# Reworked norms between layers and a rebuilt side task in a one-core transformer kernel

## The chip, the cores and the metric

One NeuronCore of a Trainium2 chip runs the whole program in one launch. The metric is the device time of one execution in microseconds; the number to predict is the median over several executions. A profiled execution gives the trace, and a program reads views out of it: the page, groups of instructions, waits, the chain that ended last, timelines and windows.

## The reference

Sequence 512, width 1024, float32. Three layers follow one another, and each has a mixer and a feed-forward part. What matters here is the first layer's end, its feed-forward part, and the second layer's start:

```python
x = x + rms_norm(merged @ w_out, norm_mix_post)          # first mixer ends
h = rms_norm(x, norm_ffn_pre)
f = square(relu(h @ w_ff1)) @ w_ff2                      # 1024 -> 4096 -> 1024
x = x + rms_norm(f, norm_ffn_post)
h = rms_norm(x, mix_norm)                                # S5 mixer begins
u = h @ ssm_w_in
# per group: x_l = a*x_{l-1} + B u_l (complex), y = Re(C x), then gelu and a gated product
```

`rms_norm` divides by the root of the mean square over the 1024 features of a token. In the kernel tokens lie along the free axis and features on the partitions, so a mean over features is a sum over partitions and over eight tiles.

## The kernel before

Activations are eight tiles of 128 features by 512 tokens. Each float32 product runs as three passes of split operands (high by high, low by high, high by low): `passes` (L226). Weights come as a stream (class `Stream`, L78): SyncE's queue loads 512 KB at a time (`wraw`, three buffers, L107), ScalarE rounds 512 columns to the high half (`whi`), and VectorE subtracts to get the low half (`wlo`), each with four buffers. For the streams named in `POOL_SPLITS` (L55: `w_s5in`, `w_gdn`) GpSimd does the subtraction. One product of a 1024-long contraction (`dense`) is 24 matmuls of 512 columns.

Tile, the framework, orders each engine's instructions at compile time by program order and its own estimate of when operands are ready, and sets the semaphores. Two engines are kept from one PSUM bank at the same time.

**Norms.** `token_sums` (L332) multiplies the tile of summed squares with a column of ones, four token blocks, and for two accumulators it interleaves them block by block; `rms_cols` (L342) turns the sums into reciprocal roots with tiny VectorE operations (`rsqrt`, L295, two steps of third order); `spread_ps` (L359) brings them back to every partition by four matmuls with the identity. A float32 matmul is two records in the trace, a transpose one.

**Norms between layers.** `post_norm` (L909) runs twice, after the first mixer and after the first feed-forward part. For each of eight blocks VectorE multiplies by the spread root and adds the old x (`x`), ScalarE makes the high half of the next input and VectorE its low half (`h`), ScalarE squares x and GpSimd adds the squares up (`pre_block`, L927). Then comes the next layer's first group of four outputs, block by block (`dense_group`, L276): 96 matmuls.

**Feed-forward part with a side task.** `ffn_relu2` (L949) does four quarters of eight 24-matmul outputs of `w_ff1` and eight of `w_ff2`. After most outputs `pump` (L191) takes one piece of `s5_prepare` (L1066), a generator that makes the S5 matrices: exact exponentials and sines, then in two halves (`s5_half`, L1120) the powers B a^n on VectorE and C a^n on GpSimd with `cmul` (L1019), six operations each on real and imaginary tiles, and for each of eight blocks (`s5_block`, L1160) expansions on ScalarE, transposes and products on TensorE, and seven doublings of a table of rotations `s5e`, six operations each. Results go to DRAM by SyncE's queue (`s5m`). The generator has 63 pieces; 61 pumps take place, and the rest is run out after the last output, before `post_norm`.

**S5 mixer.** `s5_layer` (L1235): first group, `pre_scale` (L936), then a pipeline of `s5_in`, `s5_scan`, `s5_states`, `s5_out` over eight blocks with round trips through DRAM.

Of the kernel before, what the change touches and what calls it, by code (L numbers as in the profile page):

```python
# [9 lines left out]
F32 = mybir.dt.float32  # L10
# [6 lines left out]
P = 128  # L17
# [37 lines left out]
POOL_SPLITS = ("w_s5in", "w_gdn")  # L55
# [74 lines left out]
class Kern:  # L130
# [164 lines left out]
    def rsqrt(self, m, shape, tag="", out=None):  # L295
# [6 lines left out]
        self.ts(yi, yi, 0x5DCB8400, ALU.add)  # L302
        for step in range(2):
            self.stt(a, y, (64.0 / 9.0) ** (2 - step), y, ALU.mult, ALU.mult)
            self.tt(a, a, m, ALU.mult)
            self.stt(a, a, -10.0 / 3.0, a, ALU.add, ALU.mult)
            if step == 1 and out is not None:
                self.stt(out, a, 5.0, y, ALU.add, ALU.mult)
            else:
                self.stt(y, a, 5.0, y, ALU.add, ALU.mult)  # L310
        return y if out is None else out
# [20 lines left out]
    def token_sums(self, accs, ps=None):  # L332

        if ps is None:
            ps = self.ps("s")
        for c in range(4):
            for i, acc in enumerate(accs):
                self.mm(ps[:, c:c + 1], acc[:, c * P:(c + 1) * P], self.ones[:acc.shape[0], 0:1],
                        start=(i == 0), stop=(i == len(accs) - 1))
        return ps  # L340

    def rms_cols(self, accs, n, scale=None):  # L342
# [4 lines left out]
        if scale is None:  # L347
            self.ts(m, ps[:, 0:4], 1.0 / n, ALU.mult, EPS, ALU.add)
        else:
            self.stt(m, ps[:, 0:4], 1.0 / n, scale, ALU.mult, ALU.mult)  # L350
            self.tt(m, m, scale, ALU.mult)
            self.ts(m, m, EPS, ALU.add)
        rs = self.cp.tile([P, 4], F32, name="rs_cols", tag="rs_cols", bufs=2)
        self.rsqrt(m, (P, 4), out=rs)
        if scale is not None:
            self.tt(rs, rs, scale, ALU.mult)
        return rs
# [44 lines left out]
    def first_norm(self):  # L402
# [19 lines left out]
        self.rs = self.rms_cols([acc], D)  # L422
# [486 lines left out]
    def post_norm(self, wo, accs, gain, old, gain_next, keep=True, scale=None):  # L909


        ps = self.spread_ps(self.rms_cols(accs, D, scale))
        rsb = self.cp.tile([P, T], F32, name="rsb", tag="rsb", bufs=1)
        self.act(rsb, ps)
        acc = self.tmp("acc")
# [8 lines left out]
        self.pre_acc = acc  # L924
        return xs, hs

    def pre_block(self, x, gain, acc, first, eng=None):  # L927
# [5 lines left out]
        self.sq_acc(acc, x, first, eng)  # L933
        return hi, lo

    def pre_scale(self):  # L936
        self.rs = self.rms_cols([self.pre_acc], D)
        self.rsb = self.spread(self.rs)

    def pre_norm(self, x, gain=None):  # L940
        acc = self.tmp("acc")
        hs = [self.pre_block(x[k], gain and self.col(gain, k), acc, k == 0) for k in range(KB)]
        self.pre_acc = acc
# [5 lines left out]
    def ffn_relu2(self, x, hs, gain_post, gain_next, side):  # L949
# [3 lines left out]
        rs = self.rms_cols([self.pre_acc], D)  # L953
        rs2 = self.cp.tile([P, 4], F32, name="rs2", tag="rs2", bufs=1)
        self.tt(rs2, rs, rs, ALU.mult)
# [24 lines left out]
        return self.post_norm(part, accs, gain_post, x, gain_next, scale=rs2)  # L980
# [38 lines left out]
    def cmul(self, out_r, out_i, ar, ai, br, bi, t1, t2, eng=None, conj=False):  # L1019

        eng = eng or self.nc.vector
        self.tt(out_r, ar, br, ALU.mult, eng)
        self.tt(t1, ai, bi, ALU.mult, eng)
        self.tt(out_r, out_r, t1, ALU.add if conj else ALU.subtract, eng)
        self.tt(out_i, ar, bi, ALU.mult, eng)
        self.tt(t2, ai, br, ALU.mult, eng)
        self.tt(out_i, out_i, t2, ALU.subtract if conj else ALU.add, eng)

    def exp_exact(self, out, x):

        n, r, q, e = (self.small() for _ in range(4))
        M = 12582912.0
        xc = self.small()
# [13 lines left out]
        for h in (e, n):  # L1047
            i = self.small().bitcast(I32)
# [17 lines left out]
    def s5_prepare(self):  # L1066
# [12 lines left out]
        self.exp_exact(step, ls)  # L1079
        yield  # L1080
        self.tt(t1, lr, step, ALU.mult)
        self.exp_exact(dec, t1)
# [33 lines left out]
        yield  # L1116
        for hf in range(2):
            yield from self.s5_half(hf, fr, fi, ar, ai, sn, cs)

    def s5_half(self, hf, fr, fi, ar, ai, sn, cs):  # L1120
# [5 lines left out]
        sh = [P, NP, K]  # L1126
        v = lambda t: t.rearrange("p (a k) -> p a k", k=K)
        b3 = lambda t: t[:, ps_].unsqueeze(2).to_broadcast(sh)
        tb, tc_ = ([v(t[:, 0:W]), v(t[:, W:2 * W])] for t in (self.slot("sy", name="s5t") for _ in range(2)))
# [5 lines left out]
        br, bi = v(raw[0][:, 0:W]), v(raw[0][:, W:])  # L1135
        cr, ci = v(raw[1][:, 0:W]), v(raw[1][:, W:])

        big = lambda: self.pool.tile([P, 4 * W], F32, name="s5pw", tag="s5pw", bufs=4)
# [689 lines left out]
```

## Time and profile before

| | us |
|---|---|
| median of 3 runs | 2289.0 |
| lowest, highest run | 2287.34, 2297.26 |
| the profiled execution | 2291.0 |
| its span, first to last instruction | 2289.1 |

In the profiled execution TensorE's mean granted clock is 0.977 of full speed. Start times in the rows count from the span's start. In a timeline, a line's time covers the first start to the last end of the instructions merged in it, and matmuls overlap their neighbours; the chain's times don't overlap.

### The profile page before, as it was taken

Reading aid. Unit: us, or ns where it says so; the run is one execution under the profiler, and the core shown is the slowest. Engines: PE = TensorE matmul, PEld = TensorE weight load, DVE = VectorE, ACT = ScalarE, POOL = GpSimd, SP = SyncE. Lnnn points to the kernel's source line nnn. Section 1 sums busy time; section 2 is a strip of 40 time slices with the busy share of each in tenths; the row PEclk is TensorE's granted clock in tenths of the full one; section 3 lists DMA queues with packets and bytes.
Section 4 is the critical chain, followed back from the end, with each engine's and each line's share of the span. In section 5 each row is a group of like instructions: output and inputs, shape, how many; then the busy total and the mean of one; then the engine's idle time right before and its main releaser. Section 6 shows DMA issues by size and latency. Waiting matters only on the chain.

```text
span 2289.1 us, 29097 instructions
## 1 busy us (share of the span) xinstructions
PE 2163.4 (95%) x10538; PEld 1806.3 (79%) x10538; DVE 1439.0 (63%) x2977; ACT 998.8 (44%) x1902; POOL 366.4 (16%) x400
## 2 busy tenths in 40 slices
PE   8999999999979999997789999999998899999999
PEld 6778878888867888886577788888878777888887
DVE  6678746677559557667584554355479897543542
ACT  4443336666434544463222433233357665332331
POOL 4123201111023002103451000000025541000000
PEclk9999999999989999998889999999999999999999
DMA  4211133335423444442674333333321112333332
GB/s 150 89 45 38 42 97 102 107 114 186 132 65 89 138 138 125 139 143 88 196 224 123 89 95 92 102 92 102 90 63 35 35 46 65 93 94 100 96 98 92
DMA packets 87985, 231.62 MB, mean 101 GB/s; under 512 B 10145, under 2 KB 19873, under 8 KB 87841
## 3 DMA queue, kind: packets, MB, share of 16 engines
q1 hardware_dynamic: 75168, 208.60, 30.1%
q10 hardware_dynamic: 12672, 21.16, 3.0%
q8 instruction: 83, 1.36, 0.2%
q14 instruction: 62, 0.50, 0.1%
HBM read 202.46 MB, written 27.26 MB: 100 GB/s over the span
## 4 chain that ended last, share of the span: by engine, by line
PE 76%; DVE 16%; ACT 3%; issue 2%; POOL 2%; DMA 1%; ACTq 0%; SPq 0%; DVEq 0%; POOLq 0%
PE ps_d L231 64%; PE ps_p L263 3%; PE ps_p L231 3%; PE ps_s L263 2%; PE ps_z L231 2%; DVE t L205 1%; DVE wlo L205 1%; PE ps_s L243 1%; DVE s5t L205 1%; DVE s5pw L205 1%; DVE x L212 1%; DVE h L212 1%; PE ps_p L839 1%; DVE mp L1619 1%; ACT sb_e L215 0%
## 5 line engine op out<-in xcount | busy, mean ns | idle before, releaser
L231 PE MATMUL ps_d<-h,whi 128*128 128x512 f32 (+1 forms) x3152 | 1003.8, 395 | 22.9 <-ACT h L215 10.6
L215 ACT ACTIVATE whi<-wraw 128x512 fp32r<-128x512 f32 (+1 forms) x648 | 402.4, 625 | 740.0 <-PE ps_d L231 634.9
L231 PEld LDWEIGHTS ps_d<-h,whi 128*128 128x128 f32 (+1 forms) x3152 | 595.5, 189 | 149.8 <-ACT h L215 11.6
L205 DVE TENSOR_TENSOR wlo<-wraw,whi 128x512 fp32r<-128x512 f32 x569 | 399.4, 705 | 388.4 <-ACT whi L215 383.9
L231 PE MATMUL ps_d<-h,wlo 128*128 128x512 f32 (+1 forms) x1576 | 621.6, 394 | 6.0 <-DVE wlo L205 5.1
L231 PEld LDWEIGHTS ps_d<-h,wlo 128*128 128x128 f32 (+1 forms) x1576 | 299.1, 190 | 67.9 <-DVE wlo L205 6.0
L231 PE MATMUL ps_d<-fh,wlo 128*128 128x512 f32 x608 | 237.2, 390 | 4.9 <-DVE wlo L205 4.9
L231 PE MATMUL ps_d<-fh,whi 128*128 128x512 f32 x608 | 237.6, 391 | 0.0
L231 PE MATMUL ps_d<-fl,whi 128*128 128x512 f32 x608 | 236.7, 389 | 0.0
L205 DVE TENSOR_TENSOR t<-ps_d,rsb 128x512 f32<-128x512 f32 x136 | 92.9, 688 | 127.4 <-PE ps_d L231 123.5
L231 PEld LDWEIGHTS ps_d<-fh,wlo 128*128 128x128 f32 x608 | 114.2, 188 | 30.3 <-DVE wlo L205 7.0
L231 PEld LDWEIGHTS ps_d<-fl,whi 128*128 128x128 f32 x608 | 114.1, 188 | 23.7
L231 PEld LDWEIGHTS ps_d<-fh,whi 128*128 128x128 f32 x608 | 114.2, 188 | 23.4
L205 POOL TENSOR_TENSOR wlo<-wraw,whi 128x512 fp32r<-128x512 f32 (+3 forms) x79 | 100.6, 1279 | 159.8 <-ACT whi L215 158.3
L1618 POOL MEMSET mp<- 128x128 f32 x32 | 6.6, 211 | 465.2 <-PE ps_d L231 444.3
L215 ACT ACTIVATE fh<-t 128x512 fp32r<-128x512 f32 x76 | 48.0, 631 | 66.0 <-DVE t L205 54.4
L205 DVE TENSOR_TENSOR fl<-t,fh 128x512 fp32r<-128x512 f32 x76 | 53.0, 697 | 31.9 <-ACT fh L215 30.2
L231 PE MATMUL ps_d<-whi,c 128*128 128x256 f32 (+1 forms) x224 | 53.3, 321 | 4.6 <-DVE v L212 3.6
L231 PE MATMUL ps_d<-os,whi 128*128 128x512 f32 x128 | 46.7, 420 | 8.6 <-DVE v L212 6.3
L215 ACT ACTIVATE t<-ps_d 128x512 f32<-128x512 f32 (+1 forms) x42 | 25.0, 596 | 59.0 <-PE ps_d L231 57.6
L205 POOL TENSOR_TENSOR acc<-acc,t 128x512 f32<-128x512 f32 x14 | 23.0, 1644 | 153.6 <-ACT t L215 153.5
L205 DVE TENSOR_TENSOR x<-ps_d,x 128x512 f32<-128x512 f32 x56 | 38.3, 687 | 14.4 <-PE ps_d L231 14.1
(411 smaller groups left out, 3373.1 us busy)
## 6 DMA issues: line engine op xcount, KB each, us to landing
wraw<-in_w_gu SPq DMA_DIRECT2D x88, 512.0 KB, 3.5
wraw<-in_w_ff SPq DMA_DIRECT2D x64, 512.0 KB, 3.6
wraw<-in_w_dn SPq DMA_DIRECT2D x44, 512.0 KB, 3.6
wraw<-in_w_gates SPq DMA_DIRECT2D x24, 512.0 KB, 3.6
wraw<-in_w_glu SPq DMA_DIRECT2D x16, 512.0 KB, 3.5
wraw<-in_w_sc SPq DMA_DIRECT2D x12, 512.0 KB, 3.4
gsc<-t SPq DMA_DIRECT2D x24, 256.0 KB, 2.0
sg<-gsc SPq DMA_DIRECT2D x24, 256.0 KB, 3.6
```

What stands on the lines that cost most here:

```text
L205: self.note((eng or self.nc.vector).tensor_tensor(out=out, in0=a, in1=b, op=op))
L212: (eng or self.nc.vector).scalar_tensor_tensor(out=out, in0=a, scalar=s, in1=b, op0=op0, op1=op1)
L215: self.note(self.nc.scalar.activation(out, a, fn, **kw))
L231: self.note(self.nc.tensor.matmul(ps, lhsT=a, rhs=b, start=(start and n == 0), stop=(stop and n == 3 * len(ops) - 1), skip_group_check=loose))
L243: self.note(self.nc.tensor.matmul(o, lhsT=v(h, j), rhs=x, start=(j == 0 and i == 0), stop=(j == n - 1 and i == 1)))
L263: self.nc.tensor.matmul(ps, lhsT=lhsT, rhs=rhs, start=start, stop=stop)
L839: self.nc.tensor.matmul(self.sb_at(z, i), lhsT=self.tri if j == i else self.neg, rhs=self.sb_at(s, j), start=False, stop=(j == i and n == ...
L1618: nc.gpsimd.memset(p[b][:, c0 + n:c0 + n + P], 0.0)
L1619: nc.vector.tensor_tensor_reduce(out=p[b][:, cs], in0=z[b][:, cs], in1=wide[:, 4 * P - n:], scale=1.0, scalar=-3e38, op0=ALU.add, op1=ALU. ...
```

## The change

- **Reciprocal roots.** `rms_cols` works on the plain sum (the factor 1024 goes into the constants), and `rsqrt` takes one step of third and one of second order: nine operations where there were ten. In the norm after the feed-forward part three operations on the mean and a last multiplication become one addition of a column `offset`, made early.
- **Sums and spread.** `token_sums` goes accumulator by accumulator, so the four products of the first don't stand behind the second; `spread_ps` uses transposes.
- **`post_norm`.** `keep_warm` issues ten 128-column float32 matmuls on constants after the sums and eight after the spread, in both uses. The first block's multiplication stands before ScalarE's copy of the spread. The squares and their sum leave the loop: `pre_sums` does them after the next layer's first group, on ScalarE and VectorE.
- **`w_s5in`** is split on VectorE.
- **Side task.** `cmul2` keeps real and imaginary part side by side in a tile: two multiplications over both, one subtraction, one addition, all on VectorE; GpSimd has no part in powers. Doublings 0 to 3 are made once for all 32 pairs in a new table `s5eb`; each block copies its part into `s5e` (one buffer of 128 x 1024) and does doublings 4 to 6. The pieces are cut anew: 58 pieces for 61 pumps. In a block, both transposes and the products now stand in one piece, and so do the diagonal term and the second expansions.

```diff
-POOL_SPLITS = ("w_s5in", "w_gdn")
+POOL_SPLITS = ("w_gdn",)
...
+        self.stt(a, y, 64.0 / 9.0 / (k * k), y, ALU.mult, ALU.mult)
+        self.tt(a, a, m, ALU.mult)
+        self.stt(a, a, -10.0 / 3.0, a, ALU.add, ALU.mult)
+        self.stt(y, a, 5.0, y, ALU.add, ALU.mult)
+        self.stt(a, y, -0.5 / (k * k), y, ALU.mult, ALU.mult)
+        self.tt(a, a, m, ALU.mult)
+        out = y if out is None else out
+        self.stt(out, a, 1.5, y, ALU.add, ALU.mult)
...
-        for c in range(4):
-            for i, acc in enumerate(accs):
-                self.mm(ps[:, c:c + 1], ...
+        for i, acc in enumerate(accs):
+            for c in range(4):
+                self.note(self.nc.tensor.matmul(ps[:, c:c + 1], ...
...
+    def keep_warm(self, n):
+        if n:
+            ps = self.ps("d")
+            with self.tc.issue_after(self.last_on(self.nc.tensor)):
+                for _ in range(n):
+                    self.note(self.nc.tensor.matmul(ps[:, 0:P], lhsT=self.ones, rhs=self.ident, start=True, stop=True))
...
-            self.mm(ps[:, c * P:(c + 1) * P], cols[:, c:c + 1].to_broadcast([P, P]), self.ident)
+            self.note(self.nc.tensor.transpose(ps[:, c * P:(c + 1) * P], cols[:, c:c + 1].to_broadcast([P, P]),
+                                               self.ident))
...
+        cols = self.rms_cols(accs, offset)
+        self.keep_warm(warm[0])
+        ps = self.spread_ps(cols)
+        self.keep_warm(warm[1])
         rsb = self.cp.tile([P, T], F32, name="rsb", tag="rsb", bufs=1)
-        self.act(rsb, ps)
...
             self.tt(o, o, rsb if m else ps, ALU.mult)
+            if m == 0:
+                self.act(rsb, ps)
...
-            hs.append(self.pre_block(new, self.col(gain_next, m), acc, m == 0, self.nc.gpsimd))
+            hs.append(self.pre_block(new, self.col(gain_next, m)))
...
+    def pre_sums(self, x):
+        self.pre_acc = self.tmp("acc")
+        for k in range(KB):
+            self.sq_acc(self.pre_acc, x[k], k == 0)
...
+    def cmul2(self, out, a, fr, fi, t1, t2):
+        self.tt(t1, a, fr, ALU.mult)
+        self.tt(t2, a, fi, ALU.mult)
+        self.tt(out[:, 0], t1[:, 0], t2[:, 1], ALU.subtract)
+        self.tt(out[:, 1], t1[:, 1], t2[:, 0], ALU.add)
...
+    def s5_double(self, e, k, pairs, sn, cs):
+        n, w = 1 << k, pairs.stop - pairs.start
+        o = (k + 1) * 32 + pairs.start
+        fac = [q[:, o:o + w].unsqueeze(1).unsqueeze(3).to_broadcast([P, 2, w, n]) for q in (cs, sn)]
+        self.cmul2(e[:, :, :, n:2 * n], e[:, :, :, 0:n], *fac, *self.s5_scratch(w, n))
...
-                self.cmul(pw(Cr, n), pw(Ci, n), b3(ar), b3(ai), prev[0], prev[1], *tc_, nc.gpsimd)
+                self.cmul2(pw(C, n), prev, b3(ar), b3(ai), *self.s5_scratch(NP, K))
...
+        et = self.pool.tile([P, 2 * T], F32, name="s5e", tag="s5e", bufs=1)
+        e = et.rearrange("p (x a c) -> p x a c", x=2, a=4)
+        nc.vector.tensor_copy(out=e[:, :, :, 0:16], in_=self.s5eb[:, :, m * 4:m * 4 + 4])
+        self.s5_double(e, 4, slice(m * 4, m * 4 + 4), sn, cs)
...
+        self.s5_double(e, 6, slice(m * 4, m * 4 + 4), sn, cs)
+        nc.sync.dma_start(out=dst[:, 5 * T:7 * T], in_=et)
...
         first = self.dense_group(st, hs, "ddpp")
+        self.pre_sums(x)
         self.pre_scale()
```

## Rows read from the trace of the kernel before

**Rows 1.** the page, part 1: busy us of each engine (share), instructions
```profile
PE 2163.4 (95%) x10538; PEld 1806.3 (79%) x10538; DVE 1439.0 (63%) x2977; ACT 998.8 (44%) x1902; POOL 366.4 (16%) x400
```

**Rows 2.** windows by stage; columns in the first line
```profile
core 0: us, PE busy (x) PEld busy (x) DVE busy (x) ACT busy (x) POOL busy (x), PEclk, DMA share, GB/s
...
645.00:675.00 30.00, 18.69 (x75) 15.45 (x75) 24.29 (x37) 12.41 (x22) 9.49 (x6) 0.74 0.06 18
...
675.00:1046.00 371.00, 366.08 (x1710) 304.19 (x1711) 241.70 (x678) 181.33 (x348) 52.64 (x74) 0.99 0.42 130
...
1046.00:1094.00 48.00, 34.34 (x133) 27.34 (x131) 35.55 (x84) 17.93 (x35) 19.40 (x19) 0.79 0.25 75
...
1094.00:1230.00 136.00, 103.91 (x541) 87.89 (x541) 96.73 (x119) 31.12 (x62) 58.90 (x53) 0.87 0.65 197
```

**Rows 3.** chain that ended last, first feed-forward part: start, us, what
```profile
757.23 0.87 PE ps_p L1187 x8
...
771.24 21.81 PE ps_d L231 x96
```

**Rows 4.** timeline, TensorE, first norm between layers: start, us, what, [idle <- releaser]
```profile
645.43 2.62 PE L263 MATMUL ps_s<-ones,acc 128*128 128x1 f32 x14 [1.61 <-ACT acc L215]
...
655.86 0.79 PE L231 MATMUL ps_d<-h,whi 128*128 128x512 f32 x1 [3.43 <-ACT h L215]
...
674.87 0.80 PE L231 MATMUL ps_d<-h,wlo 128*128 128x512 f32 x1 [5.12 <-DVE wlo L205]
...
687.45 0.95 PE L263 MATMUL ps_s<-ones,acc 128*128 128x1 f32 x8
```

**Rows 5.** timeline, VectorE, the same stretch
```profile
648.09 0.16 DVE L209 TENSOR_SCALAR rms_m<-ps_s 128x4 f32<-128x4 f32 x1 [2.51 <-PE ps_s L263]
...
650.08 0.16 DVE L212 SCALAR_TENSOR_TENSOR rs_cols<-rq_a,rq_y 128x4 f32<-128x4 f32 x1
...
654.30 1.41 DVE L212 SCALAR_TENSOR_TENSOR x<-wo,cols,xin 128x512 f32<-128x512 f32 x2
...
674.13 1.28 DVE L205 TENSOR_TENSOR wlo<-wraw,whi 128x512 fp32r<-128x512 f32 x2
```

**Rows 6.** windows of 1 us; columns as before, PEclk third from the end
```profile
646.00:647.00 1.00, 1.00 (x7) 1.00 (x7) 0.00 (x0) 0.00 (x0) 0.00 (x0) 0.52 0.65 74
...
659.00:660.00 1.00, 1.00 (x4) 0.83 (x3) 1.00 (x2) 0.00 (x0) 0.94 (x1) 0.65 0.00 0
...
1052.00:1053.00 1.00, 0.96 (x5) 0.96 (x6) 0.00 (x0) 0.00 (x0) 0.00 (x0) 0.61 0.68 262
```

**Rows 7.** timeline, TensorE, second norm between layers
```profile
1044.52 1.95 PE L263 MATMUL ps_p<-sz 128*128 128x128 f32 x16
...
1046.30 1.84 PE L263 MATMUL ps_s<-ones,acc 128*128 128x1 f32 x16
...
1093.68 0.95 PE L263 MATMUL ps_s<-ones,acc 128*128 128x1 f32 x8
```

**Rows 8.** timeline, VectorE, the same stretch
```profile
1066.22 1.48 DVE L205 TENSOR_TENSOR s5e<-s5e,s5et 128x256 f32<-128x256 f32 x1
...
1078.87 1.75 DVE L212 SCALAR_TENSOR_TENSOR h<-x,cols,h 128x512 fp32r<-128x512 f32 x1
```

**Rows 9.** waits of TensorE, 688 to 1044 us: total us, times, longest
```profile
PE ps_d L231 <- DVE wlo L205: 4.9, 4, 1.4
```

**Rows 10.** windows, first feed-forward part: coefficient powers, then what follows
```profile
719.00:742.00 23.00, 20.59 (x88) 16.06 (x87) 23.00 (x30) 6.57 (x12) 20.42 (x24) 1.00 0.24 70
...
742.00:902.00 160.00, 160.00 (x764) 133.95 (x763) 92.05 (x284) 81.72 (x160) 1.64 (x9) 1.00 0.45 142
```

**Rows 11.** DMA issues, 690 to 1070 us: count, KB each, us to landing
```profile
s5m<-s5e SPq DMA_DIRECT2D x16, 256.0 KB, 2.0
```

**Rows 12.** waits of SyncE's DMA queue, 690 to 1044 us
```profile
SPq L107 <- DVE wlo L205: 169.6, 46, 11.8
```

**Rows 13.** timeline, TensorE, the kernel's start
```profile
1.10 4.47 PE L263 MATMUL ps_s<-ones 128*128 128x128 f32 x24 [1.10 <-DVE ones L384]
```

More of the change, by code (lines that the diff above doesn't have):

```diff
@@ L301, in rsqrt @@
         self.ts(yi, m.bitcast(I32), 1, ALU.logical_shift_right, -1, ALU.bitwise_xor)
[L302 to L311, printed above, removed]
+        self.ts(yi, yi, self.GUESS[k], ALU.add)
+        self.stt(a, y, 64.0 / 9.0 / (k * k), y, ALU.mult, ALU.mult)
[6 more added lines that the diff above has]
+        self.stt(out, a, 1.5, y, ALU.add, ALU.mult)
+        return out
     def sq_acc(self, acc, src, first, eng=None):
@@ L922, in post_norm, with pre_block @@
             xs.append(new)
-            hs.append(self.pre_block(new, self.col(gain_next, m), acc, m == 0, self.nc.gpsimd))
-        self.pre_acc = acc
+            hs.append(self.pre_block(new, self.col(gain_next, m)))
         return xs, hs
-    def pre_block(self, x, gain, acc, first, eng=None):
+    def pre_block(self, x, gain):
         hi, lo = self.slot("h", F32R), self.slot("h", F32R)
@@ L932, in pre_block @@
             self.split_scaled(hi, lo, x, gain)
-        self.sq_acc(acc, x, first, eng)
         return hi, lo
+    def pre_sums(self, x):
+        self.pre_acc = self.tmp("acc")
+        for k in range(KB):
+            self.sq_acc(self.pre_acc, x[k], k == 0)
     def pre_scale(self):
-        self.rs = self.rms_cols([self.pre_acc], D)
+        self.rs = self.rms_cols([self.pre_acc])
         self.rsb = self.spread(self.rs)
     def pre_norm(self, x, gain=None):
-        acc = self.tmp("acc")
-        hs = [self.pre_block(x[k], gain and self.col(gain, k), acc, k == 0) for k in range(KB)]
-        self.pre_acc = acc
+        self.pre_acc = self.tmp("acc")
+        hs = []
+        for k in range(KB):
+            hs.append(self.pre_block(x[k], gain and self.col(gain, k)))
+            self.sq_acc(self.pre_acc, x[k], k == 0)
         return hs
@@ L1017, in small, with exp_exact @@
         return self.sm_tile[:, o:o + 32 * n]
[L1019 to L1031, printed above, removed]
+    def cmul2(self, out, a, fr, fi, t1, t2):
[3 more added lines that the diff above has]
+        self.tt(out[:, 1], t1[:, 1], t2[:, 0], ALU.add)
+    def exp_exact(self, out, x, scratch):
+        n, r, q, e, xc, *two = scratch
         M = 12582912.0
-        xc = self.small()
         self.ts(xc, x, 100.0, ALU.min, -115.0, ALU.max)
@@ L1046, in exp_exact @@
         self.tt(n, n, e, ALU.subtract)
-        for h in (e, n):
-            i = self.small().bitcast(I32)
+        for h, t in zip((e, n), two):
+            i = t.bitcast(I32)
             self.ts(i, h, 127.0, ALU.add, 8388608.0, ALU.mult)
@@ L1078, in s5_prepare @@
         step, dec, t1, t2 = (self.small() for _ in range(4))
-        self.exp_exact(step, ls)
+        scratch = [self.small() for _ in range(7)]
+        self.exp_exact(step, ls, scratch)
         yield
         self.tt(t1, lr, step, ALU.mult)
-        self.exp_exact(dec, t1)
+        self.exp_exact(dec, t1, scratch)
         self.tt(t1, dec, dec, ALU.mult)
@@ L1125, in s5_half @@
         W = NP * K
[L1126 to L1129, printed above, removed]
+        v = lambda t: t.rearrange("p (x a k) -> p x a k", x=2, k=K)
+        b3 = lambda t: t[:, ps_].unsqueeze(1).unsqueeze(3).to_broadcast([P, 2, NP, K])
         raw = [self.slot("sy", name="s5raw") for _ in range(2)]
@@ L1154, in s5_half @@
         for b in range(4):
-            for _ in self.s5_block(hf * 4 + b, b, Br, Bi, Cr, Ci, cr, ci, sn, cs):
+            if b == 0:
+                next(c_pw)
+            for _ in self.s5_block(hf * 4 + b, b, B, C, v(raw[1]), sn, cs):
                 if b == 0:
```

105 lines of the change are left out of this document (48 added, 57 removed).

## The prediction

> **What bounds the kernel now.** I read the page's busy shares first, then windows by stage, then the chain, and last the timelines of two engines around the two norms between layers. TensorE is busy 95% of the span [rows 1], so a gain has to come from the few places where it stands or runs slowly. The stages show where [rows 2]: around the first norm it is busy 18.7 of 30 us at a mean granted clock of 0.74, around the second 34.3 of 48 at 0.79, in the S5 pipeline 103.9 of 136 at 0.87. In the feed-forward part between them it is busy 366.1 of 371 us: little is to be had there, whatever the side task costs the others.
>
> A first group of a layer is 96 matmuls, which take 21.8 us at full clock [rows 3]. From the first norm's waiting sums to the end of that group 42.0 us go by (645.43 to 687.45) [rows 4]; from the last output's end in the feed-forward part to the end of the S5 group it is 49.2 (1044.52 to 1093.68) [rows 7]. So some 20 and 25 us stand around the matmuls. Three things fill them. Small VectorE operations run one by one, 0.2 us each: eleven from 648.09 to 650.25 [rows 5]. The loop on VectorE is slowed where GpSimd works beside it: a half that takes 0.67 takes 1.75, a 256-wide doubling 1.48 [rows 5, 8]. And the clock is at its lower level (1.2 GHz) part of the time: at 646 us it falls after TensorE had stood for 1.6 us, and rises at 659.6, 3.8 us after the group began [rows 4, 6].
>
> **First norm.** Unchanged: the second accumulator is ready at 645.43 [rows 4]. The four products of the first one now stand before that, so eight records are left behind it: 0.9 us at full clock (16 in 1.84 [rows 7]), 1.5 at the lower one (14 in 2.62 [rows 4]). Then ten small operations instead of eleven, 2.0 us. Beside them run the ten fillers: the start of the kernel has twelve of their size in 4.47 us at the lower clock [rows 13], so ten take 3.7; at full clock a record costs 0.115, so 2.3. The spread is four transposes, 0.44 (eight in 0.87 [rows 3]), with 0.15 of hand-over. If the clock holds, VectorE starts at 645.43 + 0.9 + 2.0 + 0.6 = 648.9. If it falls at 646.0 as before and rises 3.8 us later, the fillers end at about 650.3 and the loop starts at 650.9; if it doesn't rise in time, at 651.8.
>
> The loop is eight blocks of one multiplication (0.60, as the paired subtractions at 674.13) and two three-operand operations (0.67, [rows 5]), without GpSimd beside it: 15.5 us. TensorE, fed every 1.9 us, needs 2.73 for a block, so it would be the bound. But VectorE also makes `wlo`, and the order shown by the trace puts the fifth block's `wlo` behind nearly the whole loop: 674.13, after the last x, with TensorE standing 5.12 us for it [rows 4, 5]. I take that order as kept. It is ready 14.7 us after the loop starts; TensorE has done its four prepared blocks about 13 us after, stands 1.7, and needs 10.9 for the other four. The group ends 25.6 us after the loop's start: 674.5 with the clock held, 676.5 with the fall, 677.4 at the worst. The gain is 13.0, 11.0 or 10.0. I take **11.0**, since in the nearest row the clock is down before the first filler could begin.
>
> The fillers take `d` banks whose readers are done, and what is queued behind them on TensorE is the spread, then the group; the price of that is in the three cases. ScalarE's copy of the spread now waits for the first multiplication, which only the second block needs: nothing, as VectorE has the first block's addition meanwhile.
>
> The Trainium skill, TensorE: Matmul & The Clock Gate, section "What's actually happening", has the activity monitor's window run free of the kernel, so that a fall can come at another moment in another run. By that 674.5 and 676.5 are both open, 2 us apart; no run here tells which.
>
> **Second norm.** The last output ends at 1044.52, and the side task's tail follows on TensorE [rows 7]. That tail (16 records and four transposes, 2.2 us) moves ahead of the last outputs, where TensorE is full: the end comes at 1046.7. As before the first norm 1.6 us pass until the second accumulator is there; then 0.9, ten operations at 0.2 (fourteen before), 0.6: the loop starts at 1051.8. Gone from this stretch is what ran between: the doublings of the last block, one of them 1.48 us long [rows 8], and GpSimd's sums and splits. GpSimd's `wlo` of this stream becomes VectorE's, and with the order above the same wait of 1.7 us appears here, new. The group ends 25.6 us after: 1077.4, against 1093.68: **16.3**. Here I take the clock as held: before, it stayed full from 1044.5 to 1052 [rows 6], though with the tail as work. If it falls, 2 to 3 us less.
>
> Behind both groups stand the squares and sums: eight on ScalarE, seven additions of 0.60 on VectorE, 4.2 us. VectorE has the time while TensorE does the last four blocks, so they cost nothing as long as the loop holds its 15.5 us; if not, the sums wait, TensorE's queue with them, and in the S5 part the spread root that every `s5_in` needs: up to 4 us at each place. There the way from group to spread root itself gets an operation and four records shorter: **0.6**.
>
> **Side task.** TensorE waits for VectorE 4.9 us in four waits [rows 9], all where powers run on both engines: VectorE is full 23.0 of 23 us, GpSimd 20.4 [rows 10]. With four operations in place of six, a product is about 1.9 us uncontended (two of 512 columns at 0.60 [rows 5], two of half that, which I estimate at 0.35), and sixteen are 30 us spread over 61 pumps; the largest piece (two products, a copy and a doubling) is 4.7 us of an interval of 5.5, a quarter of the 96 matmuls. Outside the powers VectorE was busy 92 of 160 us, doublings included [rows 10], 3.1 in an interval; so this piece overshoots by some 2, under the cover of four prepared `wlo`, 10.9 us of TensorE. So the 4.9 come back. Against it: three PSUM tiles in one piece on two `p` banks, so the products wait for ScalarE's copy of the first transposes. No row shows that wait; where these pieces stood apart, TensorE was busy 160.0 of 160 us [rows 10], which is the lower end, 0; the upper is a copy of 512 columns and its hand-over, 1 us as ScalarE's part of the 1.6 before the sums [rows 4]. As other matmuls can be ordered between, I take 0.2 for each of eight blocks: 1.5. Net **3.4**, ends 4.9 and -3.1.
>
> **The rest.** 16 other reciprocal roots, 0.2 us each, a third of them where someone waits: **1.2** (0 to 3.2). Spreads at three other norms, four records less each: **1.3** (0 to 1.5). `w_s5in` on VectorE in the pipeline, eight splits: 4.8 us on an engine busy 96.7 of 136 [rows 2], against eight fewer on GpSimd, each of which could slow a VectorE operation by 1 us. Between -4.8 and +8 I take 0, as chain and relief share the same stretch.
>
> The Trainium skill, TensorE: Matmul & The Clock Gate, section "Terms", gives the transpose mode as four times faster for float32. The row has it at twice (0.87 for eight against 1.84 for sixteen). By the page a spread would be 0.2 us shorter, six times, and the sum 1.3 lower.
>
> **Sum.** 11.0 + 16.3 + 0.6 + 3.4 + 1.2 + 1.3 = 33.8. The profiled execution took 2291.0, so 2257.2; it lies 2.0 above the median of the runs, which leaves **2255**.
>
> **Rivals.**
> *Fillers that don't hold the clock.* It falls in both norms, the fillers run at the lower level and the spread stands behind them. For it: the fall at 646.0 precedes them, and twelve such records at the start ran at the lower clock [rows 13]. Against: rises within 3.8 us of work. Price: 1 and 3 us: 2259.
> *The gain given back in S5.* The sums come late or the additional splits sit on the chain of scans: 4 + 4.8 us, and 4 more at the first norm: 2268. For it: VectorE is on that chain, and the sums now depend on it. Against: the additions fit beside TensorE's last four blocks.
> *The loop meets its splits.* The framework's order changes and `wlo` comes in time at both norms (3.4), GpSimd's absence quickens S5 (up to 8): 2246.
> *Slower.* The single `s5e` buffer: the copy for block m+1 waits until block m's 512 KB are in DRAM, and VectorE's queue, `wlo` first, stands behind it. The stores land in 2.0 us [rows 11], but on SyncE's queue a weight load can wait up to 11.8 us [rows 12] and hold a store behind it. The cover is 10.9. If each of seven copies lost 7 us, the 3.4 would not come and 49 would be lost: 2255 + 3 + 49 = 2307. It begins to cost at a landing 16.4 us after the doubling (an interval and the cover) and turns the sign at about 22; the rows speak for 2 to 14.
> *It doesn't do what it says*, a piece of the side task still standing in the second norm: 5 us, 2260.
>
> **Chances.** Forecast and tail piece (2250 to 2262) 0.52, clock 0.13, given back 0.18, better 0.12, slower 0.05 (with others of its sign). The ends of the unknown costs reach 2240 and 2272, and this range leaves less than 2 in 10 out. A measurement of this kernel can tell about 0.5%, 11 us. Faster by more (under 2277.6): 0.91; within: 0.06; slower: 0.03.
>
> **What would show it.** In the profile after: a first group ending about 25 us after the loop's start; no GpSimd beside the loops; the window clock at 1.0 through the second norm; no side-task operation behind the last output; TensorE full from 688 on; a wait on `wlo` in the middle of both groups. Wrong it would be if halves still took 1.7 us without GpSimd, if TensorE stood for the sums behind a group, if pieces with three PSUM tiles showed waits on ScalarE, or if the S5 part grew by what the norms gave.

## The result, and the profile after

The changed kernel takes 2261.92 us (median; 2261.87 to 2263.37), the kernel before 2288.55 in the runs beside it: the ratio is 0.9877, with an interval of 0.9852 to 0.9902. So it is faster by 1.2%, clear of the runs' spread, 7 us behind the forecast of 2255 and inside the range. The profiled execution of after took 2261.87 us (span 2260.0, mean granted clock 0.981), that of before 2291.0: 29.1 between the two traces. In two later sets of runs the changed kernel took 2260.7 and 2258.95, beside 2289.1 and 2288.29 of before.

Stages are cut here where TensorE starts the products of a norm's sums (the second accumulator's at the first norm; at the second norm the first accumulator's, which before the change stand together with the second's and now 1.6 us ahead of them). The page's first part and windows at these cuts, of the kernel after; the columns are us, busy us (instructions) of TensorE, its weight load, VectorE, ScalarE, GpSimd, then the granted clock and DMA. The order is mixer, first norm to the end of its group, feed-forward part, second norm to the end of its group, S5 part, second feed-forward part, MLA, third:

```profile
PE 2161.9 (96%) x10586; PEld 1808.0 (80%) x10586; DVE 1416.0 (63%) x2778; ACT 1001.7 (44%) x1902; POOL 278.1 (12%) x308
```

```profile
33.66:647.77 614.11, 588.35 (x3083) 494.05 (x3081) 417.27 (x750) 302.82 (x553) 101.06 (x119) 0.99 0.29 95
647.77:679.15 31.38, 29.47 (x144) 25.11 (x145) 27.27 (x51) 16.69 (x27) 3.50 (x9) 0.95 0.21 68
679.15:1033.70 354.55, 354.45 (x1673) 294.61 (x1672) 224.67 (x517) 178.59 (x344) 0.00 (x0) 1.00 0.40 134
1033.70:1066.34 32.64, 30.41 (x154) 25.97 (x153) 25.87 (x47) 16.96 (x31) 0.36 (x4) 0.95 0.32 107
1066.34:1285.56 219.22, 186.70 (x910) 155.60 (x909) 146.77 (x188) 64.18 (x118) 48.47 (x46) 0.92 0.50 157
1285.56:1642.10 356.54, 355.66 (x1573) 292.00 (x1572) 174.22 (x300) 125.90 (x221) 1.78 (x4) 1.00 0.29 93
1642.10:1917.34 275.24, 248.83 (x1437) 215.96 (x1436) 227.39 (x675) 173.75 (x412) 107.21 (x111) 0.94 0.15 48
1917.34:2260.00 342.66, 338.93 (x1501) 280.30 (x1499) 154.15 (x235) 105.55 (x167) 0.00 (x0) 1.00 0.30 96
```

Against before, by the same cuts (the third to the fifth are differences of starts in [rows 4] and [rows 7], the others are read from the same timeline of before):

| stage | before | after | difference | predicted |
|---|---|---|---|---|
| start | 34.02 | 33.66 | -0.4 | in "the rest" |
| mixer | 611.41 | 614.11 | **+2.7** | in "the rest" |
| first norm and group | 42.02 | 31.38 | -10.6 | -11.0 |
| feed-forward part | 358.85 | 354.55 | -4.3 | |
| second norm and group | 47.38 | 32.64 | -14.7 | with the line above -19.7 |
| S5 part | 223.93 | 219.22 | **-4.7** | -0.6 |
| second feed-forward part | 357.21 | 356.54 | -0.7 | in "the rest" |
| MLA | 270.93 | 275.24 | **+4.3** | in "the rest" |
| third feed-forward part | 343.35 | 342.66 | -0.7 | in "the rest" |

"The rest" was put at -2.5 and came to +5.2. The first norm came out as worked out, the second together with the feed-forward part. First TensorE's timeline around the first norm (start, us, what, idle before and its releaser), which answers [rows 4]:

```profile
645.89 0.95 PE L341 MATMUL ps_s<-ones,acc 128*128 128x1 f32 x8
647.77 1.17 PE L341 MATMUL ps_s<-ones,acc 128*128 128x1 f32 x8 [0.94 <-ACT acc L215]
648.81 3.99 PE L365 MATMUL ps_d<-cst,ones 128*128 128x128 f32 x20
652.63 0.60 PE L371 MATMUL ps_s<-cst,rs_cols 128*128 128x128 f32 x4
...
655.55 0.50 PE L231 MATMUL ps_d<-h,whi 128*128 128x512 f32 x1 [0.53 <-ACT h L215]
...
669.00 0.50 PE L231 MATMUL ps_d<-h,wlo 128*128 128x512 f32 x1 [1.37 <-DVE wlo L205]
...
679.15 0.95 PE L341 MATMUL ps_s<-ones,acc 128*128 128x1 f32 x8
```

VectorE's timeline of that stretch, answering [rows 5], and windows of 1 us with the granted clock, answering [rows 6]:

```profile
650.77 0.16 DVE L212 SCALAR_TENSOR_TENSOR rs_cols<-rq_a,rq_y 128x4 f32<-128x4 f32 x1
653.27 0.69 DVE L205 TENSOR_TENSOR wo<-wo,ps_s 128x512 f32<-128x512 f32 x1 [2.34 <-PE ps_s L371]
...
663.68 0.75 DVE L212 SCALAR_TENSOR_TENSOR h<-x,cols,h 128x512 fp32r<-128x512 f32 x1
...
668.26 0.69 DVE L205 TENSOR_TENSOR wlo<-wraw,whi 128x512 fp32r<-128x512 f32 x1
```

```profile
647.00:648.00 1.00, 0.23 (x2) 0.23 (x3) 0.69 (x1) 0.72 (x2) 0.00 (x0) 1.00 0.03 8
648.00:649.00 1.00, 1.00 (x9) 1.00 (x9) 0.02 (x1) 0.00 (x0) 0.00 (x0) 0.78 0.11 16
649.00:650.00 1.00, 1.00 (x5) 1.00 (x6) 0.83 (x6) 0.00 (x0) 0.00 (x0) 0.50 0.81 254
652.00:653.00 1.00, 1.00 (x11) 1.00 (x11) 0.00 (x0) 0.00 (x0) 0.00 (x0) 1.00 0.00 0
```

The reader is to see four things. The root is done at 650.93, but the four transposes wait until 652.63, behind fillers that run at 1.2 GHz: the clock fell in the window that starts at 648 and is back at 652. The loop starts 5.50 us after the second sums (forecast 5.5: 645.43 to 650.9). A half takes 0.75 with GpSimd away. And the fifth block's `wlo` stands behind the loop, so that TensorE waits 1.37 us for it (forecast 1.7). The group ends 25.9 us after the loop's start (forecast 25.6). At the second norm the same wait on `wlo` is there in TensorE's timeline:

```profile
1056.21 0.50 PE L231 MATMUL ps_d<-h,wlo 128*128 128x512 f32 x1 [1.42 <-DVE wlo L205]
```

### The profile page after: what moved, and what is told of

The parts are those of the page before. It is cut to its first block, busy times and chain, and to the rows that moved or that the text cites. A ratio compares the mean times of both kernels' runs of the same rounds, so it can differ in the third digit from the quotient of the medians.

```text
span 2260.0 us, 28842 instructions
## 1 busy us (share of the span) xinstructions
PE 2161.9 (96%) x10586; PEld 1808.0 (80%) x10586; DVE 1416.0 (63%) x2778; ACT 1001.7 (44%) x1902; POOL 278.1 (12%) x308
## 4 chain that ended last, share of the span: by engine, by line
PE 81%; DVE 11%; ACT 3%; issue 2%; DMA 2%; POOL 1%; SPq 0%; ACTq 0%; DVEq 0%; POOLq 0%
PE ps_d L231 68%; PE ps_p L263 3%; PE ps_p L231 3%; PE ps_z L231 2%; PE ps_s L243 1%; DVE t L205 1%; DVE wlo L205 1%; PE ps_s L263 1%; DMA matB<-s5m 1%; PE ps_p L848 1%; ACT sb_e L215 1%; DVE h L212 0%; DVE s5t L205 0%; DVE mp L1646 0%; DVE tok L205 0%
## 5 line engine op out<-in xcount | busy, mean ns | idle before, releaser
L205 DVE TENSOR_TENSOR wlo<-wraw,whi 128x512 fp32r<-128x512 f32 x585 | 409.5, 703 | 381.2 <-ACT whi L215 375.8
L205 POOL TENSOR_TENSOR wlo<-wraw,whi 128x512 fp32r<-128x512 f32 (+3 forms) x63 | 78.4, 1249 | 107.1 <-ACT whi L215 106.9
L205 DVE TENSOR_TENSOR fl<-t,fh 128x512 fp32r<-128x512 f32 x76 | 52.6, 692 | 32.8 <-ACT fh L215 30.7
L231 PE MATMUL ps_d<-whi,c 128*128 128x256 f32 (+1 forms) x224 | 55.3, 331 | 12.5 <-DVE v L212 10.2
L231 PEld LDWEIGHTS ps_d<-whi,c 128*128 128x128 f32 x224 | 39.7, 201 | 15.7 <-DVE v L212 11.6
```

The costliest lines, as they stand in the source:

```text
L205: self.note((eng or self.nc.vector).tensor_tensor(out=out, in0=a, in1=b, op=op))
L231: self.note(self.nc.tensor.matmul(ps, lhsT=a, rhs=b, start=(start and n == 0), stop=(stop and n == 3 * len(ops) - 1), skip_group_check=loose))
```

## The experiments

Each kernel is the changed one with one edit, unless the text says otherwise. In a stage the clock can matter as much as an edit, so the table has for each profiled execution the us of a stage and, behind the stroke, the full-clock time lost in it: the sum of (1 - granted clock) over windows of 1 us. e1 to e4 were run beside the kernel before alone, e6, e8 and e9 also beside e5, e10 and e11 beside e12.

| kernel | mixer | first norm | feed-forward | second norm | S5 | MLA | median us |
|---|---|---|---|---|---|---|---|
| before | 611.4 / 3.4 | 42.0 / 10.2 | 358.9 / 0 | 47.4 / 10.2 | 223.9 / 18.8 | 270.9 / 6.8 | 2288.55 |
| after | 614.1 / 5.1 | 31.4 / 1.7 | 354.6 / 0 | 32.6 / 1.7 | 219.2 / 17.1 | 275.2 / 15.4 | 2261.92 |
| e5_again | 613.6 / 5.1 | 31.4 / 1.7 | 354.6 / 0 | 31.4 / 0 | 218.1 / 15.3 | 275.0 / 15.4 | 2260.7 |
| e12_again | 615.1 / 6.8 | 31.4 / 1.7 | 354.6 / 0 | 32.7 / 1.7 | 216.2 / 15.4 | 274.9 / 15.4 | 2258.95 |
| e1_old_root | 613.6 / 6.8 | 31.3 / 1.7 | 354.6 / 0 | 31.4 / 0 | 217.6 / 13.6 | 273.1 / 10.2 | 2258.53 |
| e2_no_fill | 615.4 / 6.8 | 32.3 / 5.1 | 354.6 / 0 | 34.3 / 5.1 | 213.7 / 11.9 | 274.9 / 15.4 | 2261.74 |
| e3_pool_in_loop | 613.8 / 5.1 | 40.1 / 5.1 | 354.6 / 0 | 41.5 / 5.1 | 212.2 / 13.7 | 275.3 / 15.4 | 2274.33 |
| e4_s5in_pool | 614.3 / 3.4 | 31.3 / 1.7 | 354.6 / 0 | 30.8 / 0 | 215.1 / 13.7 | 275.0 / 15.3 | 2257.18 |
| e6_old_side | 614.4 / 6.8 | 31.4 / 1.7 | 358.9 / 0 | 38.6 / 1.7 | 213.1 / 13.6 | 275.0 / 15.4 | 2268.52 |
| e8_both | 610.7 / 3.4 | 31.4 / 1.7 | 354.5 / 0 | 32.1 / 1.7 | 217.4 / 15.3 | 270.9 / 6.8 | 2254.4 |
| e9_gap_fill | 615.2 / 6.8 | 29.7 / 0 | 354.5 / 0 | 31.4 / 0 | 218.7 / 18.8 | 275.2 / 15.4 | 2258.4 |
| e10_best | 612.2 / 5.1 | 29.7 / 0 | 354.6 / 0 | 30.7 / 0 | 218.6 / 20.5 | 273.2 / 10.2 | 2253.94 |
| e11_ff1_pool | 611.9 / 3.4 | 30.9 / 0 | 365.5 / 6.8 | 30.8 / 0 | 213.5 / 13.7 | 273.5 / 8.5 | 2265.54 |

**Where the mixer and MLA lost time: e1_old_root.**

```diff
     def rsqrt(self, m, shape, tag="", out=None, k=1):
...
+        if k == 1:
+            self.ts(yi, yi, 0x5DCB8400, ALU.add)
+            for step in range(2):
+                self.stt(a, y, (64.0 / 9.0) ** (2 - step), y, ALU.mult, ALU.mult)
+                self.tt(a, a, m, ALU.mult)
+                self.stt(a, a, -10.0 / 3.0, a, ALU.add, ALU.mult)
+                self.stt(y, a, 5.0, y, ALU.add, ALU.mult)
+            return y
```

> The 16 reciprocal roots outside the norms (heads of the mixer, latents and heads of MLA) go back to the old ten operations; the roots of the norms keep the new nine. Theory: with one operation fewer in each, the framework put the work of the GDN core and of MLA in another order, and this is where the mixer lost 2.7 us (611.4 to 614.1) and MLA 4.3 us (270.9 to 275.2). Then both stages come back to within 1 us of the kernel before, and the time is about 2255 (6 to 7 us under the changed kernel). Rival: the order there was moved by something else (the token sums, the spread by transposes, the sums that stand elsewhere); then the stages keep 614 and 275, and 16 operations of 0.2 us that are added give 2262 to 2265.

Measured: 2258.53 us (2255.67 to 2261.89), a range that overlaps the changed kernel's, so the whole time doesn't show the gain; the stages do. MLA takes 273.07, the mixer 613.57, neither fully back. Of TensorE's 3,070 records from the first sums to those of the first norm (the spread's left out), and of its 1,295 from MLA's last group of sums to the third feed-forward part, each stands in the same place as in the kernel before; in the changed kernel 521 and 299 of them stand elsewhere. So the shorter root did reorder the work. The clock in MLA, windows of the whole stage, first of before, then of after, of e1 and of e8 (which has the old order too):

```profile
1674.82:1945.75 270.93, 244.07 (x1438) 210.84 (x1437) 231.80 (x686) 173.25 (x412) 108.89 (x111) 0.97 0.17 49
```

```profile
1642.10:1917.34 275.24, 248.83 (x1437) 215.96 (x1436) 227.39 (x675) 173.75 (x412) 107.21 (x111) 0.94 0.15 48
```

```profile
1638.37:1911.44 273.07, 245.62 (x1437) 212.82 (x1436) 231.56 (x685) 173.59 (x412) 108.90 (x111) 0.96 0.17 49
```

```profile
1635.54:1906.45 270.91, 244.01 (x1437) 210.82 (x1436) 231.40 (x685) 173.41 (x412) 108.88 (x111) 0.97 0.17 49
```

VectorE works 4.4 us less in the changed kernel's MLA (227.39 against 231.80), TensorE stands about as long (26.4 and 26.9, us less busy us), but is busy 4.8 us longer at a lower clock. TensorE's waits in MLA differ too, of before and of after (us in total, times, longest):

```profile
PE ps_d L231 <- DVE v L212: 9.9, 6, 3.2
```

```profile
PE ps_d L231 <- DVE v L212: 11.5, 7, 3.1
PE ps_d L231 <- ACT tm L215: 2.4, 3, 0.9
```

In the new order TensorE waits seven times for `v` instead of six, and three times for `tm` (0.9 in one wait before). That these waits bring the longer stretches of low clock is not shown: e11, which has the old order, also waits seven times for `v` and loses 8.5. The clock falls some 37 us after the stage's start in both, in windows of 1 us: before it is back after 4 us (1711 to 1715), in the changed kernel after 11 (1679 to 1690). e5 and e12 tell whether that is chance.

**The changed kernel again: e5_again and e12_again.** No edit.

> The changed kernel itself once more, unaltered, as the measure for the others of this call and as a second trace of the same instructions. Theory one, the order costs: MLA is at 275 us with five stretches of low clock again, since its order is the same; what differs between two executions is only where single falls lie (in the mixer, at the second norm, in the S5 part), each worth up to 1.7 us. Theory two, chance: MLA comes out as short as before (271) in this execution. Time 2259 to 2264.

> The changed kernel unaltered, as the measure for the two others of this call: 2259 to 2263, MLA 275 with about 15 us of lost clock once more.

Measured: 2260.7 (2258.68 to 2264.93) and 2258.95 (2257.74 to 2260.72). MLA is at 275.04 and 274.88, with 15.4 us of clock lost each time. All eight profiled executions with the new order (after, e2 to e6, e9, e12) lie between 274.87 and 275.31 and lose 15.3 or 15.4; all five with the old one (before, e1, e8, e10, e11) lie between 270.91 and 273.54 and lose 6.8 to 10.2. So in MLA it is the order, not chance: 2.7 us between the means (275.1 and 272.3). In the mixer the two sets touch (613.6 to 615.4 against 610.7 to 613.6); the means differ by 2.5 (614.5 and 611.9), so there the cost of the order is less sure. The first of the two theories holds. What chance does is seen at the second norm, where the same program took 32.64, 31.37 and 32.65, as the clock fell, held and fell.

**Fillers: e2_no_fill and e9_gap_fill.**

```diff
-... warm=(10, 8))
+... warm=(0, 0))
```

> Both post norms without their 18 fillers. In the changed kernel the spread's transposes stood 1.9 us (first norm) and 1.05 us (second) behind fillers, most of which ran at the lower clock. Theory: the fillers bring the full clock to the group (in the changed kernel it rose 1.3 us before the first group and just after the loop's start of the second), without them the loop starts 1 to 2 us sooner but the first four blocks run at the lower clock; as the wait on wlo, 14.7 us after the loop's start, binds anyway, the group's end moves by -2 to +1 us at each norm: 2258 to 2264. Rival: without fillers the clock stays low through the wait and into the second half of the groups: +4 us at each, 2270.

Measured: 2261.74 (2260.88 to 2267.77), no difference from after. The low clock lasts longer (5.1 us lost at each norm, against 1.7 or none), and the groups end later, by 0.9 us at the first norm and by 1.6 to 2.9 at the second, which is beyond the expected -2 to +1; but the S5 part is 2.4 to 5.5 shorter. The rival of a clock that stays low, 2270, falls.

```diff
     def token_sums(self, accs, ps=None):
...
+            if i == 0 and len(accs) > 1:
+                self.keep_warm(4)
...
-... warm=(10, 8))
+... warm=(6, 8))
```

> Four of the ten fillers of each norm between layers move into the gap in which TensorE waits for the second accumulator (0.94 and 0.66 us); six and eight stay. Theory: the fall at the first norm (a few tenths of a us after the second sums start) follows on that gap; with work in it the clock holds at both norms, six fillers at 0.23 us end before VectorE's root, and the groups end 2 to 3 us (first) and 1 to 2 us (second) sooner: 2257 to 2259. Rival: the gap alone doesn't decide it, the nine operations of the root that follow count too; the clock falls all the same at the first norm: 2260 to 2262.

Measured: 2258.4 (2256.73 to 2260.59). TensorE's timeline of e9 at the first norm and two windows of 1 us:

```profile
647.67 0.94 PE L341 MATMUL ps_s<-ones,acc 128*128 128x1 f32 x8
648.48 1.14 PE L367 MATMUL ps_d<-cst,ones 128*128 128x128 f32 x8
649.56 1.05 PE L341 MATMUL ps_s<-ones,acc 128*128 128x1 f32 x8
650.47 1.58 PE L367 MATMUL ps_d<-cst,ones 128*128 128x128 f32 x12
652.74 0.62 PE L373 MATMUL ps_s<-cst,rs_cols 128*128 128x128 f32 x4 [0.68 <-DVE rs_cols L212]
```

```profile
649.00:650.00 1.00, 1.00 (x10) 0.87 (x9) 0.69 (x1) 0.51 (x1) 0.00 (x0) 1.00 0.02 8
650.00:651.00 1.00, 1.00 (x11) 1.00 (x10) 0.32 (x2) 0.00 (x0) 0.00 (x0) 1.00 0.45 61
```

With work in the gap the clock holds at the first norm, the transposes wait for VectorE instead of for fillers, and the stage takes 29.69 in place of 31.37. The same holds in e10 and e11, which have this edit; in all nine traces with the new sums and without it the clock fell there, 0.6 to 1.6 us after the second sums began. So the fall follows on the gap of 0.94 us ahead of the second sums. At the second norm, with a gap of 0.66 us, the clock held too (31.35), but so it did in e1, e4 and e5 without this. The groups gain less than expected (1.7 at the first norm, nothing against e5 at the second), and the whole time doesn't show the gain: its range overlaps that of e5, run beside it, and over the whole kernel e9 loses 44.5 us of full clock, the three traces of the changed kernel 41.2 to 44.6.

**GpSimd beside the loop: e3_pool_in_loop.**

```diff
     def post_norm(self, ...):
...
+            if m == 0:
+                acc = self.tmp("acc")
+            self.sq_acc(acc, new, m == 0, self.nc.gpsimd)
+        self.pre_acc = acc
...
-        self.pre_sums(x)
```

> The squares and sums of the next norm go back into the post norm's loop on GpSimd, all else as in the changed kernel. Theory: what freed the two groups is GpSimd's absence beside VectorE; with it a three-operand operation of 512 columns goes from about 0.7 back to some 1.7 us, the loop from 15.7 to over 25 us, and each group ends 5 to 10 us later: 2272 to 2282, with nothing gained elsewhere. Rival: the groups were freed by the other edits (no side work, the clock) and GpSimd's sums cost little, as the matmuls cover them: 2262 to 2266.

Measured: 2274.33 (2271.75 to 2275.43), as the theory had it. VectorE's and GpSimd's timelines of e3 in the first norm's loop:

```profile
657.78 0.74 DVE L212 SCALAR_TENSOR_TENSOR h<-x,cols,h 128x512 fp32r<-128x512 f32 x1
658.45 1.78 DVE L212 SCALAR_TENSOR_TENSOR x<-wo,cols,xin 128x512 f32<-128x512 f32 x1
660.16 1.77 DVE L212 SCALAR_TENSOR_TENSOR h<-x,cols,h 128x512 fp32r<-128x512 f32 x1
...
663.55 0.74 DVE L212 SCALAR_TENSOR_TENSOR h<-x,cols,h 128x512 fp32r<-128x512 f32 x1
```

```profile
657.97 3.42 POOL L205 TENSOR_TENSOR acc<-acc,t 128x512 f32<-128x512 f32 x2 [122.96 <-PE ps_d L231]
661.65 1.42 POOL L205 TENSOR_TENSOR acc<-acc,t 128x512 f32<-128x512 f32 x1 [0.27 <-ACT t L215]
```

The low half `h` takes 0.74 where GpSimd stands and 1.77 where it adds. The first norm takes 40.06, 8.7 more than in the changed kernel: of the 10.6 gained there, 8.7 are GpSimd's absence, the clock that it costs included (5.1 us lost against 1.7). The second takes 41.54 (+8.9).

**The side task: e6_old_side.** The products, halves and blocks of before and its slot counts are put back.

```diff
-    def cmul2(self, out, a, fr, fi, t1, t2):
+    def cmul(self, out_r, out_i, ar, ai, br, bi, t1, t2, eng=None, conj=False):
...
-... sy=7, sz=7, so=2):
+... sy=8, sz=7, so=3):
```

> The side task of the feed-forward part as before (six-operation products on VectorE and GpSimd, all seven doublings per block, 63 pieces with the last ones behind the feed-forward part), with the new norms. By the prediction's steps TensorE gets back waits of 4.9 us in the powers, and 2.2 us of records and the last block's doublings stand in the second norm again, beside its loop: +8 to +14, 2270 to 2276, all of it in the feed-forward part (+3 to +5) and the second norm (+5 to +9). Rival: the new norm alone is worth it and the side task hides as before: within 3 us of the changed kernel.

Measured: 2268.52 (2265.59 to 2269.62), 7.8 over e5, run beside it, and just short of the expected 2270 to 2276. Waits of TensorE in the feed-forward part of e6:

```profile
PE ps_d L231 <- DVE wlo L205: 5.0, 5, 1.4
```

It waits 5.0 us, where the changed kernel is busy 354.45 of 354.55. The part takes 4.4 us more, the second norm 7.2, both as expected, but the S5 part 5.0 less (213.07), and that was not. e3, with its late second group, has the same: 212.21. Over the traces of after and of the experiments the S5 part is shorter where the second group ends later: 215.1 to 219.2 us in the eight where it ends by 1068.7, 212.2 to 213.7 in the four where it ends at 1071.2 or later (e2, e3, e6, e11). So part of what is gained ahead of the S5 part seems to be given back in it. One wait differs: for the load of `U`, 16 to 17 us into the part, TensorE stands 1.8 to 3.0 us in the three traces of the changed kernel and not at all in e3 and e6. The rest these runs don't settle.

**Splits on GpSimd: e4_s5in_pool and e11_ff1_pool.**

```diff
-POOL_SPLITS = ("w_gdn",)
+POOL_SPLITS = ("w_s5in", "w_gdn")
```

> The splits of w_s5in go back to GpSimd, in the S5 group and in the pipeline, all else as in the changed kernel. Theory: the S5 part became 4.7 us shorter (223.9 to 219.2) because GpSimd no longer works beside VectorE's scan chain; then it goes back to about 224, and the group of the second norm gets 1 to 4 us later, since the loop has GpSimd beside it again: 2266 to 2270. Rival: the S5 part gained by the norm's shorter way and by the single load of the blocks' data (512 KB in fewer pieces); then it stays at 219 and the wait of 1.4 us on wlo goes: 2260 to 2262.

Measured: 2257.18 (2255.95 to 2259.7). The theory falls: the S5 part does not go back to 224 but to 215.12, and the rival's 219 and 2260 to 2262 don't come either. Second norm and S5 part together take 245.9, against 248.8 to 251.9 in the three executions of the changed kernel. So in this one trace GpSimd's splits were 3 to 6 us better than VectorE's, where the prediction took zero between -4.8 and +8; e8 and e10 below don't show it again, so a gain from them is not shown.

e11 is e10 (below) with the stream of the first norm's group on GpSimd too.

```diff
-POOL_SPLITS = ("w_s5in", "w_gdn")
+POOL_SPLITS = ("w_ff1", "w_s5in", "w_gdn")
```

> As e10_best, and the splits of w_ff1 (the stream of the first norm's group) on GpSimd too. Theory: the wait of 1.4 us on wlo in the middle of the first group goes, since wlo no longer stands behind VectorE's loop; but GpSimd works beside the loop again for four to eight splits: between -1.4 and +3 at the first norm, and nothing in the feed-forward part, which TensorE fills (354.5): within 3 us of e10_best. Rival: GpSimd beside VectorE slows the side task's products so that TensorE waits in the feed-forward part: +5 or more there.

Measured: 2265.54 (2261.57 to 2267.5), the rival. The feed-forward part takes 365.50. TensorE's waits in it, and at its start:

```profile
PE ps_p L263 <- ACT s5o L215: 4.5, 1, 4.5
PE ps_s L349 <- DVE acc L205: 2.2, 1, 2.2
```

These are the two waits that the prediction named as signs of being wrong, the `p` banks and the sums behind a group. In the changed kernel neither is there; they appear as soon as GpSimd works beside VectorE, and the clock falls behind each (6.8 us lost in the feed-forward part). The second wait ends at 677.16, with the first norm's stage; the first is in the feed-forward part. VectorE's timeline shows how it comes about:

```profile
762.38 0.74 DVE L205 TENSOR_TENSOR s5pw<-s5t 128x256 f32<-128x256 f32 x2
...
766.16 2.77 DVE L205 TENSOR_TENSOR s5pw<-s5t 128x256 f32<-128x256 f32 x2
768.86 0.68 DVE L212 SCALAR_TENSOR_TENSOR t<-ps_d,t 128x512 f32<-128x512 f32 x1
```

The last two operations of a product take 0.74 us alone and 2.77 at 766.16, where GpSimd makes two splits (765.45 to 768.66). VectorE's `t` stands behind them, ScalarE stands 3.20 us for `t`, and its copy `s5o`, next in its order, is what TensorE waits for.

**What gains, together: e8_both and e10_best.** e8 has the edits of e1 and e4, e10 also that of e9.

> The old ten-operation roots outside the norms and the splits of w_s5in on GpSimd, together. TensorE's order in the mixer and in MLA is then that of the kernel before, instruction by instruction. Theory: MLA 273 (old order) and second norm with S5 part 246 (the wait on wlo gone) add up: 2251 to 2255. Rival: the two gains of the first call were single falls of the clock that lay elsewhere by chance; then 2258 to 2262 as the changed kernel.

> The three edits that each gained, together: old ten-operation roots outside the norms (e1), the splits of w_s5in on GpSimd (e4), four fillers in the gap ahead of the second sums (e9). If they add up: mixer 611 to 613, first norm 29.7 with the clock held, second norm with S5 part 246 to 249, MLA 271 to 273, so 2247 to 2253, 9 to 14 under the changed kernel in the same call. If what was gained was chance of single falls of the clock: 2255 to 2261.

Measured: e8 2254.4 (2249.7 to 2263.37). e10 2253.94 (2252.01 to 2254.97), ratio to before 0.9848 (0.9829 to 0.9867), 5.0 under the changed kernel run beside it (e12, 2257.74 to 2260.72). e8's MLA and mixer are those of before to within 0.8 us; the second norm and S5 part of both (249.5 and 249.3) don't show e4's full gain again, and e10 lost the most clock of all in the S5 part (20.5). So e8 came out at the upper end of what was expected, and e10 just above it (2253.94 against 2247 to 2253, 5.0 under the changed kernel where 9 to 14 were expected): the three gains don't fully add up. e10 is faster than both kernels, and its runs don't overlap those of either.

## Why the prediction was right, and where it was not

**First norm, 11.0: right.** 10.6 came. The clock fell in all three traces of the changed kernel, as assumed: in two of them 0.2 and 0.4 us before the first filler, in e5 0.7 after it, and the loop starts 5.5 us after the second sums in each. The length of a filler at the lower clock was taken from the kernel's start, where no row shows the clock (the windows there read 1.00, and only the records' length, 0.19 us against 0.115, speaks for the lower level); the ten fillers took 3.99 us here, most of it at the lower clock, where 3.7 were forecast. e9 shows the other end, 12.3 (42.02 to 29.69), where 13.0 was given for a held clock.

**Second norm and side task, 16.3 and 3.4: right, by terms that erred in opposite ways.** Together 19.0 came (20.3 in e5). From the first sums to the group's end the forecast is 30.7 (1046.7 to 1077.4); it took 31.4 with the clock held and 32.6 where it fell, so the assumption that it holds was good in one of three traces, at 1.3 us a fall where the prediction had 2 to 3. The Trainium skill, TensorE: Matmul & The Clock Gate, section "What's actually happening", has the activity monitor's window run free of the kernel. These three executions of one program agree with it. By the cuts above the side task gave 4.3; in the forecast's terms, in which the tail moves from the norm into the feed-forward part, 4.7 (357.07 and 2.2 of tail against 354.55), as the 1.5 us of waits for `p` banks didn't appear.

**S5 part, 0.6: too small by 4.** The first scan starts 21.1 us after the group's end, before it was 24.8; the first of after, then of before:

```profile
1087.45 2.27 DVE L1349 TENSOR_TENSOR_SCAN s5sr<-rho,s5br 128x512 f32<-128x512 f32 x1 [0.20 <-POOL s5br L205]
```

```profile
1118.51 2.27 DVE L1322 TENSOR_TENSOR_SCAN s5sr<-rho,s5br 128x512 f32<-128x512 f32 x1 [0.22 <-POOL s5br L205]
```

That is 3.7 of the 4.7. The step counted one operation and four records of the root's way. What it left out is what follows on it: with the splits on GpSimd again (e4, e8, e10) the scan starts at 22.0 to 22.3, against 20.2 to 21.1 in the three traces of the changed kernel, so 1 to 2 us are theirs. The rest is seen at the load of `U`: TensorE's first wait for it ends 17.0 us after the group's end, before it was 18.9, and takes 3.0 us in place of 6.3. The waits of before, then of after (us in total, times, longest):

```profile
PE ps_p L263 <- DMA U<-s5u: 7.3, 2, 6.3
```

```profile
PE ps_p L263 <- DMA U<-s5u: 5.5, 2, 3.0
```

What of this is the earlier root, the store of `ut` or the load itself no run here takes apart. The forecast put the splits at 0 and had nothing for the load; that these 4 us made up for half of the next miss was luck.

**The rest, 2.5: wrong in sign, the step that failed.** Sixteen reciprocal roots were costed as "0.2 us each, a third of them where someone waits". But a shorter chain doesn't only end earlier: the framework puts the work of the mixer and of MLA in another order, which costs 2.5 and 2.7 us by the means of the two sets of executions, in place of 1.2 gained. That is 6.4 of the 7.7 us between -2.5 and +5.2; another 1.8 lies in the two traces taken, as MLA and mixer differ by 7.0 between them and by 5.2 between the means. The start and the two other feed-forward parts gave 0.4, 0.7 and 0.7, where the term for the spreads had 1.3, which takes 0.5 off again.

**The offset of 2.0: chance.** The profiled execution of before lay 2.0 above its median; that of after lies at its own (2261.87 and 2261.92), that of e5 1.7 below and that of e12 1.8 above. So of the 7 us by which the forecast missed, 4.7 are the stages' (33.8 against 29.1) and 2.0 this offset. The medians differ by 26.6, 28.4 and 29.3 in the three sets.

So by the traces: 33.8 less 0.4 (first norm) less 0.7 (second norm and side task) less 7.7 (the rest) plus 4.1 (S5) is 29.1. That the time lies inside the range rests on the norms and the side task, which gave 29.7 of their 30.7.

**The rivals.** The first, fillers that don't hold the clock, came in part: in two of the three traces of the changed kernel the clock fell at both norms, and the spread stood behind fillers, 1.7 us at the first norm of after. Its price was smaller: nothing at the first norm against a forecast that had counted the fall, and 1.3 at the second where it had 3. The fillers shorten the low clock, but the whole time is the same without them (e2). The others did not come. The single `s5e` buffer cost nothing: TensorE is busy 354.45 of 354.55 us. In S5 nothing was given back against before, but beside e6 and e3 the changed kernel's S5 part is 3 to 7 us longer.

## What to carry to other kernels

A chain made shorter can cost time where the framework orders instructions by estimated times: compare the order of the bounding engine's instructions in both programs before an edit is costed at its operations' durations. A gap of 0.94 us ahead of a norm's last sums was enough for the clock to fall here, in nine of nine traces, and work in the gap kept it up in three of three, where more work behind the gap did not; but look at the whole time too, which didn't show that gain by itself. And of the first norm's gain most (8.7 of 10.6 us) was one engine kept away from another.

## What was not expected of the hardware

The same order of TensorE's instructions in MLA ran at 270.91 with 6.8 us of clock lost and at 273.07 with 10.2; differences of 2 us in a stage are within what one program does. The other order lost 15.3 or 15.4 in each of eight executions, with the first fall 36.8 to 37.3 us into the stage in all of them. TensorE's standing time was about the same (26.4 and 26.9 us); what the order changed was the clock at which it was busy.
